# Attention with a written-out TensorE order, its transposes in two PSUM pools, and the bias sums one unit ahead

## The chip, the cores and the metric

The kernel runs on one core of one Trainium2 chip. The metric is device time in microseconds of one execution; less is better. A core has five engines that run side by side, each with its own queue of instructions in a fixed order: TensorE (PE: matrix products and transposes; PEld is its weight load), VectorE (DVE), ScalarE (ACT), GpSimd (POOL), and SyncE (SP), which here only starts DMA transfers. Work memory is SBUF; TensorE writes its results to PSUM, which has eight banks of 128 x 512 float32.

## What is computed

One layer of a streaming encoder on 1024 frames with width 1024, float32. Cut to what matters here:

```python
h = rmsnorm(x, pre_norm_mix) * (1.0 + scale_m) + shift_m
proj = h @ w_in            # q_lat, kv_lat, k_idx, w_idx, z, xbc, dt_raw, g_a, g_b
y_a = sparse_mla_attention(...) @ w_o_attn
y_b = ssd_mixer(z, xbc, dt_raw, ...) @ w_o_ssd
mix = (sigmoid(g_a) * y_a + sigmoid(g_b) * y_b) @ w_out
x = x + gate_m * rmsnorm(mix, post_norm_mix)
...
f = (silu(u_gate) * u_up) @ w_ffn_out
x = x + gate_f * rmsnorm(f, post_norm_ffn)
```

The attention has 16 heads. An indexer scores all keys for each query, the 256 best admissible keys are kept, and

```python
logits = einsum('bqhc,bqkc->bhqk', q_b, kv_sel) * scale + bias
probs = softmax(where(valid, logits, -inf))
o = einsum('bqhk,bqkc->bqhc', probs, kv_sel)
o = einsum('blhc,hcd->blhd', o, w_uv)
```

The xbc columns go through a causal convolution of four taps and a Silu before the state-space mixer. g_a and z are the columns of the two gates.

## The kernel before

The kernel is written against a framework that traces it in program order, then plans: a planner simulates the engines in time, gives an instruction that stands earlier in the program the higher priority, and so fixes each engine's queue at compile time. [...] `in_order(engines)` (line 103) chains the instructions traced inside it on the named engines, so that the planner must keep their program order there; other instructions may still be put between them. PSUM is split into a pool `ps` of five banks (`bank`) and a pool `pd` of three (`bank_d`).

The stages, in order: projections and the indexer's scores; the ranking, which finds the 256 best keys of each query by bisection on VectorE and ScalarE and writes the masks `mk` (line 700); attention; the state-space mixer; the merge of the two branches; the feed-forward part.

**Filler.** The remaining columns of w_in need nothing but h: 32 tiles of 128 columns for the convolution, 16 for z, 8 for g_a. One tile is 8 row tiles x 3 products (each float32 operand is split into a high and a low part) x 2 halves of the frames = 48 matmuls of 128x512 into the tile `pw` (line 224). The string FILL lists them: x or X a group of four convolution tiles, z and a one gate tile each. A convolution tile is read from PSUM by ScalarE (line 909) and three taps by VectorE (lines 912 to 914); a Silu follows on ScalarE (line 919). With X the Silus of two tiles are done together.

**Attention** is 8 head pairs (hp) times 4 units u of 256 queries, taken in the order u = 0, 2, 1, 3: 32 units. `att_scores` makes queries (`puq`, 12 matmuls; split into qh on ScalarE, line 735, and ql on VectorE, line 736). Then come four steps, one for each query tile t and head hh: GpSimd adds bias and mask into `nm` (line 748, once per t), TensorE makes scores into one or two banks `plg` (line 764), VectorE adds nm or mk and takes the maximum (line 773), ScalarE takes the exponential and its sum (line 776), VectorE the reciprocal (line 777). `att_out` of the unit before transposes the probabilities, one turn for each key tile j (`pt`, line 797), copies them to SBUF (`pc`: VectorE for odd j, ScalarE for even j), multiplies them with the values (`po`, line 813) and scales by the spread reciprocals (r2, lines 784 and 809). `weave` alternates steps of `att_scores` with steps of `att_out`. Beside each unit, `ada_next` makes one column of the modulation: weights `adaw` by DMA, products on GpSimd (lines 315, 316), a sum on VectorE (line 317), a small matmul `adap`.

In the program, hp 0 to 2 stand first, then FILL, then hp 3 to 7. No order is forced (`ATT_ORDER` is empty). Transposes of hp 0 to 2 take banks of `ps`, the later ones of `pd`.

Of the kernel before, what the change touches and what calls it, by code (L numbers as in the profile page):

```python
# [10 lines left out]
F32 = mybir.dt.float32  # L11
# [6 lines left out]
P = 128  # L18
# [12 lines left out]
LOWEST = -BIGGEST  # L31
QC = 256
ORDERED = (mybir.EngineType.PE, mybir.EngineType.Activation, mybir.EngineType.DVE)
FILL = "xxxxx" + "z" * 16 + "a" * 8 + "XXX"
HP_FIRST = 3
LEAD = 1.5
U_ORDER = (0, 2, 1, 3)
ATT_ORDER = ()
NCH = L // QC
EARLY = 18  # L40

# [24 lines left out]
def build(tc, a, dbg=None, stop=99, slots=None):  # L66
# [658 lines left out]

    qscale = KV_RANK ** -0.5

    def att_scores(u, uq, nb, out):

        pq = bank("puq")  # L730
        for hh in range(2):
# [9 lines left out]
        for t in range(2):  # L741
            i = 2 * u + t
            n = (i + 1) * P
            near = max(0, n - 256)
            nw = n - near
            nm = Q("nm", (P, 2, 256))
            mk = MK[i][:, near:n] if i in MK else dmask[:, 256 - nw:256]
            G.tensor_tensor(nm[:, :, 0:nw], nb[:, :, 256 - nw:256], mk[:, None, :].to_broadcast([P, 2, nw]), op=OP.add)
            a_ = max(256, n - 512) if n > 512 else 0
            for hh in range(2):  # L750
                st = [QQ[x][:, 256 * hh + 128 * t:256 * hh + 128 * t + 128] for x in range(2)]
                if u >= 2:
                    lg = R("lg")
                else:
                    if hh == 0:
                        pair = R("lg")
                    lg = pair[:, half(hh)]
                mx = sm.tile([P, 4], F32, name="mx", bufs=6)
                pb_ = {}
                for o_, w_ in ((a_, n - a_),) + (((0, a_),) if a_ else ()):  # L760
                    p = bank("plg")
                    w2 = max(w_, 256)
                    for x, (qi, ki) in enumerate(P3):
                        T.matmul(p[:, 0:w2], st[qi], KVT[ki][:, o_:o_ + w2], start=x == 0, stop=x == 2)  # L764
                    pb_[o_] = p
                parts = [(a_, near, n, nm[:, hh, 0:nw])]
                if near > a_:
                    parts.append((a_, a_, near, MK[i][:, a_:near]))
                if a_:
                    parts.append((0, 0, a_, MK[i][:, 0:a_]))  # L770
                m = 3e38
                for x, (o_, s_, e_, add) in enumerate(parts):
                    V.tensor_tensor_reduce(lg[:, s_:e_], pb_[o_][:, s_ - o_:e_ - o_], add, op0=OP.add, op1=OP.min,  # L773
                                           scale=-1.0, scalar=m, accum_out=mx[:, x:x + 1])
                    m = mx[:, x:x + 1]
                S.activation(lg[:, 0:n], lg[:, 0:n], AF.Exp, scale=-1.0, bias=m, accum_out=mx[:, 3:4])  # L776
                V.reciprocal(rr[:, 2 * t + hh:2 * t + hh + 1], mx[:, 3:4])
                out[hh, t] = lg
                yield

    def att_out(hp, u, vt, PR):

        r2 = sm.tile([P, 2, 2, 64], F32, name="r2", bufs=1)
        G.tensor_copy(r2, PR["rr"].rearrange("p (t h) -> p t h", t=2)[:, :, :, None].to_broadcast([P, 2, 2, 64]))
        po = bank("po")
# [4 lines left out]
        def turn(j):  # L790
            ts = (0, 1) if j < last else (1,)
            sl = slice(ts[0], 2)
            pt = (bank if hp < HP_FIRST else bank_d)("pt")
            ptv = pt.rearrange("p (h t n) -> p h t n", h=2, t=2)
            for hh in range(2):
                for t in ts:
                    T.transpose(ptv[:, hh, t, :], PR[hh, t][:, j * P:(j + 1) * P], ident)  # L797
            pc = Q("pc").rearrange("p (h t n) -> p h t n", h=2, t=2)
            if j % 2:
                V.tensor_copy(pc[:, :, sl], ptv[:, :, sl])  # L800
            else:
                S.activation(pc[:, :, sl], ptv[:, :, sl], AF.Copy)
            parts[j] = pc, sl
# [39 lines left out]

    att = {}

    def attention(steps, last, beside=lambda: None):

        for s_ in steps + [None] * last:
            nxt = iter(())
            if s_ is not None:  # L850
                hp, u = s_
                if u == U_ORDER[0]:
                    vt = vp.tile([P, NT, P], F32, name="vt", bufs=1)
                    SP.dma_start(vt, d_v[hp])
                    att["w"] = small_weights(a["w_uq"][hp]), vt, load_bias(hp)
                uq, vt, nb = att["w"]
                PR = {}
                nxt = att_scores(u, uq, nb, PR)
            prev = att.get("prev")
            if prev is None:  # L860
                weave(nxt, 5, iter(()), 0)
            else:
                weave(nxt, 5 if s_ else 0, att_out(*prev), 2 * prev[1] + 3, lead=LEAD)
            if s_ is not None:
                att["prev"] = (hp, u, vt, PR)
            beside()
# [3 lines left out]
    def ada_next():  # L870
# [3 lines left out]
            ada_col(*late.pop(0))  # L874
        if j is not None:
            late.append(ada_slow(j))

    if stop != 3:
        attention([(hp, u) for hp in range(HP_FIRST) for u in U_ORDER], 0, ada_next)
        if stop == 4:  # L880
            attention([(hp, u) for hp in range(HP_FIRST, 8) for u in U_ORDER], 1)
    if stop == 4:
        for k in range(KT):
            for b in BS:
                t = EV("attd")
                SP.dma_start(t, d_att[k][:, half(b)])
                dump("attn", t, (k, slice(None), half(b)))
        ctx.close()
        return


    def wide(c):
        W.plan(col_tile(a["w_in"][c]))
# [25 lines left out]
            S.activation(t, t, AF.Silu)  # L919
            SP.dma_start(dst, t)  # L920

    def conv_group(g, n):

        tiles = ((16 + g, d_bc[g, 0]), (24 + g, d_bc[g, 1]), (2 * g, d_xs[2 * g]), (2 * g + 1, d_xs[2 * g + 1]))
        for i in range(0, 4, n):
            outs = [o for t in tiles[i:i + n] for o in conv(*t)]
            if n > 1:
                with in_order(mybir.EngineType.Activation):
                    conv_out(outs[::-1])
            else:  # L930
                conv_out(outs)

    n_x, n_z, n_a = iter(range(GROUPS)), iter(range(16)), iter(range(8))
    for kind in FILL:
        if kind in "xX":
            conv_group(next(n_x), 2 if kind == "X" else 1)
        elif kind == "z":
            t = next(n_z)
            gate(1 + t, d_z[t], AF.Silu)
        elif stop != 3:  # L940
# [119 lines left out]
    def beside():  # L1060

        for t in range(8):
            W.plan(col_tile(a["w_in"][57 + t]))
            w = wpieces(ks8)
            for b in BS:
                p = bank_d("pw")
                yield from dense_steps(p, b, w, Hs)
                o = EV("g")
                S.activation(o, p, AF.Copy)
                SP.dma_start(d_gb[t][:, half(b)], o)  # L1070
                yield
        AT = [([None, None], [None, None]) for _ in range(KT)]
        for b in BS:
            for k in range(KT):
# [474 lines left out]
```

## Time and profile before

| | us |
|---|---|
| median of three runs | 2464.63 |
| the three runs | 2464.63, 2466.57, 2458.57 |
| the profiled execution, own time | 2461.74 |
| its span, first to last instruction | 2459.9 |
| mean granted TensorE clock in it | 0.985 |
| ranking's last mask written | 678.4 |
| first and last transposes of attention | 675.0, 1147.7 |

The page of the profile gives for each engine its busy time and share of the span, then the chain of work that ended last. A row of a window gives the stretch, its length, each engine's busy time with its number of instructions, and then PEclk, the share of the TensorE clock that was granted. A row of waits names who waited, for whom, and then the total us, the number of times, and the longest. A row of the timeline gives start and duration in us, engine, line, operation and out<-in, and in brackets the idle time before it with what ended it; matmuls of one line that follow one another are merged (x16). A row of groups gives count | busy us, mean ns of one | idle us before it and what ended that. Matmuls are pipelined, so their durations overlap: what one costs is read from start to start.

### The profile page before, as it was taken

The page shows a single profiled execution, that of the slowest core. Times are in us where ns is not written, and L with a number is a line of the kernel's source. Part 1 is how long each engine was busy: PE and PEld are TensorE (multiplying, and loading weights), DVE is VectorE, ACT ScalarE, POOL GpSimd, SP SyncE. Part 2 cuts the span into 40 slices and gives each one's busy share as a digit, 9 for nine tenths or more (in the row PEclk, how much of TensorE's full clock was granted, in tenths as well). Part 3 has the DMA queues.
Part 4 walks back from the last instruction along what each step waited for, and adds up shares of the span by engine and source line. Part 5 has one row for each costly group of instructions (what it writes and reads, how often), then busy time and mean ns, then how long its engine had stood idle before and what let it go on. Part 6 is the DMA issues. An engine that isn't in the chain of part 4 may idle for free.

```text
span 2459.9 us, 34979 instructions
## 1 busy us (share of the span) xinstructions
PE 2387.0 (97%) x11940; PEld 1933.8 (79%) x11940; DVE 1447.2 (59%) x2956; ACT 1209.1 (49%) x2327; POOL 1079.3 (44%) x877
## 2 busy tenths in 40 slices
PE   7999999999899999999999999999999999999997
PEld 5788888888788887777776777888777888888886
DVE  4566775599745656765558667365476666542211
ACT  3446665567444555555656555454454222344432
POOL 2722112222234344563335345656576555444564
PEclk8999999999999999999999999999999999999999
DMA  7224212522222332223668775664465444354453
GB/s 268 90 86 126 69 65 79 162 86 98 91 63 87 107 97 94 89 82 124 214 215 261 231 231 194 210 201 160 159 216 172 154 159 146 120 163 142 146 164 113
DMA packets 219746, 352.79 MB, mean 143 GB/s; under 512 B 22016, under 2 KB 86192, under 8 KB 219568
## 3 DMA queue, kind: packets, MB, share of 16 engines
q1 hardware_dynamic: 218848, 349.99, 44.1%
q8 instruction: 94, 1.54, 0.3%
q14 instruction: 84, 0.69, 0.1%
q10 hardware_dynamic: 720, 0.58, 0.1%
HBM read 266.31 MB, written 87.32 MB: 144 GB/s over the span
## 4 chain that ended last, share of the span: by engine, by line
PE 76%; DVE 9%; DMA 5%; ACT 4%; issue 3%; POOL 2%; SPq 1%; POOLq 0%; ACTq 0%; DVEq 0%
PE pw L224 17%; PE p L1281 14%; PE pfo L1413 9%; PE plg L764 4%; PE pos L224 4%; PE poa L234 3%; PE pot L224 3%; PE po L813 3%; PE pt L797 3%; PE pw L234 3%; PE prel L581 3%; PE puq L224 2%; DVE junk L634 2%; ACT junk L636 1%; PE pp L370 1%
## 5 line engine op out<-in xcount | busy, mean ns | idle before, releaser
L150 POOL TENSOR_TENSOR wlo<-wraw,whi 128x512 fp32r<-128x512 f32 x242 | 329.1, 1362 | 606.9 <-ACT whi L149 551.0
L1281 PE MATMUL p<-xh,wr 128*128 128x512 f32 x880 | 274.4, 391 | 3.1 <-DVE g L1331 3.1
L149 ACT ACTIVATE whi<-wraw 128x512 fp32r<-128x512 f32 x242 | 150.9, 626 | 195.0 <-issue 45.1
L1413 PE MATMUL pfo<-a,fwh 128*128 128x512 f32 (+1 forms) x684 | 208.6, 386 | 0.9 <-DVE a L245 0.9
L1275 POOL TENSOR_TENSOR wr<-a,wr 128x512 fp32r<-128x512 f32 x110 | 151.0, 1386 | 103.2 <-ACT wr L1274 70.4
L1281 PEld LDWEIGHTS p<-xh,wr 128*128 128x128 f32 x880 | 165.9, 189 | 38.0 <-DVE g L1331 3.5
L1281 PE MATMUL p<-xl,wr 128*128 128x512 f32 x440 | 171.7, 390 | 0.0
L245 POOL TENSOR_TENSOR fwl<-fw,fwh 128x512 fp32r<-128x512 f32 x92 | 113.4, 1236 | 115.9 <-ACT fwh L244 111.1
L1413 PEld LDWEIGHTS pfo<-a,fwh 128*128 128x128 f32 x684 | 127.5, 188 | 27.8 <-DVE a L245 1.8
L776 ACT ACTIVATE lg<-lg,mx 128x256 f32<-128x256 f32 (+7 forms) x128 | 98.2, 769 | 75.6 <-DVE mx L773 74.5
L1413 PE MATMUL pfo<-a,fwl 128*128 128x512 f32 (+1 forms) x342 | 131.8, 385 | 0.0
L1274 ACT ACTIVATE wr<-a 128x512 fp32r<-128x512 f32 x110 | 67.7, 628 | 123.3 <-PE p L1281 94.1
L315 POOL TENSOR_TENSOR adaw<-adaw,cs 128x512 f32<-128x512 f32 x64 | 66.7, 1043 | 117.9 <-DMA adaw<-ada_w 117.8
L244 ACT ACTIVATE fwh<-fw 128x512 fp32r<-128x512 f32 x92 | 54.5, 594 | 124.2 <-PE pfo L1413 95.5
L1281 PE MATMUL p<-h2h,wr 128*128 128x512 f32 x352 | 112.3, 396 | 0.0
L636 ACT ACTIVATE junk<-acc,cand__2203 128x1024 bf16<-128x1024 f32 (+2 forms) x96 | 86.2, 898 | 45.1 <-DVE cand__2203 L679 28.1
L224 PE MATMUL pos<-yw,whi 128*128 128x512 f32 x256 | 101.9, 398 | 3.3 <-DVE yw L1124 3.3
L224 PE MATMUL pos<-yh,whi 128*128 128x512 f32 x256 | 101.4, 396 | 2.9 <-ACT yh L1123 2.9
L224 PE MATMUL pos<-yh,wlo 128*128 128x512 f32 x256 | 101.5, 396 | 0.7 <-POOL wlo L150 0.7
L587 DVE SCALAR_TENSOR_TENSOR acc<-rel,widx,acc 128x384 f32<-128x384 f32 (+2 forms) x90 | 87.1, 988 | 24.5 <-ACT rel L582 24.3
L582 ACT ACTIVATE rel<-prel 128x512 f32<-128x512 f32 (+3 forms) x160 | 77.2, 524 | 47.7 <-PE prel L581 44.2
L1281 PEld LDWEIGHTS p<-xl,wr 128*128 128x128 f32 x440 | 83.0, 189 | 17.3
(567 smaller groups left out, 6869.1 us busy)
## 6 DMA issues: line engine op xcount, KB each, us to landing
wraw<-w_in SPq DMA_DIRECT2D x130, 256.0 KB, 2.9
a<-w_ffn_in SPq DMA_DIRECT2D x124, 256.0 KB, 3.3
fw<-w_ffn_out SPq DMA_DIRECT2D x80, 256.0 KB, 2.7
adaw<-ada_w SPq DMA_DIRECT2D x64, 256.0 KB, 2.8
al<-d_ac SPq DMA_DIRECT2D x32, 512.0 KB, 5.7
wraw<-w_o_ssd SPq DMA_DIRECT2D x64, 256.0 KB, 3.2
al<-d_a SPq DMA_DIRECT2D x44, 256.0 KB, 5.3
d_a<-g SPq DMA_DIRECT2D x40, 256.0 KB, 2.4
```

The lines of the kernel that those rows point to most:

```text
L149: behind(S.activation(hi[:, :kt], raw[:, :kt], AF.Copy))
L150: behind(G.tensor_tensor(lo[:, :kt], raw[:, :kt], f(hi[:, :kt]), op=OP.subtract))
L224: T.matmul(o, wt[:, k0 + i, :], xs[k][xi][b][:, sl], start=pi == 0 and i == 0 and wt is hi and xi == 0, stop=pi == len(pcs) - 1 and i == l ...
L234: T.matmul(o, wt[:, k0 + j, :], xs[k][xi][b], start=i == 0, stop=i == 23)
L245: (lo_eng or V).tensor_tensor(lo, src, f(hi), op=OP.subtract)
L587: V.scalar_tensor_tensor(acc[i][:, 0:n], rel[:, 0:n], ws, acc[i][:, 0:n], op0=OP.mult, op1=OP.add)
L636: S.activation(jk, y, AF.Sign, scale=-1.0, bias=a_, accum_out=o)
L764: T.matmul(p[:, 0:w2], st[qi], KVT[ki][:, o_:o_ + w2], start=x == 0, stop=x == 2)
L776: S.activation(lg[:, 0:n], lg[:, 0:n], AF.Exp, scale=-1.0, bias=m, accum_out=mx[:, 3:4])
L1275: G.tensor_tensor(w[:, 1], src, f(w[:, 0]), op=OP.subtract)
L1281: T.matmul(p, w[:, wi, i], X[x][i][xi], start=start and i == 0 and k == 0, stop=i == 3 and k == 2, skip_group_check=True)
L1413: T.matmul(p, w[wi][:, k - k0], xs[k][xi][:, sl], start=k == 0 and i == 0, stop=k == FT - 1 and i == 2)
```

## The change

Attention becomes one stretch of 32 units behind the filler, and TensorE's order in it is the program's. FILL loses its last three groups X (12 tiles, convolution groups 5 to 7). `woven` issues them in steps of six matmuls, three steps to a unit, through `conv_steps`; that handles one half of the frames at a time, in one pd bank, and takes the last three frames of the first half along in `ends`. Within a unit the order is: a step of scores, then a quarter of the turns of the unit before, and so on, then the last step of att_out; filler steps are spread evenly. Even turns j use a `pd` bank, odd ones a `ps` bank. VectorE copies the turns with j % 3 = 1, ScalarE the others. `biases` makes both sums of a unit while the unit before is running, with the load of the bias at the head pair's first unit. The exponential's sum goes straight into rr, and one reciprocal per unit replaces four.

```diff
-FILL = "xxxxx" + "z" * 16 + "a" * 8 + "XXX"
-HP_FIRST = 3
-LEAD = 1.5
+FILL = "xxxxx" + "z" * 16 + "a" * 8
+WOVEN = "XXX"
 U_ORDER = (0, 2, 1, 3)
-ATT_ORDER = ()
...
-    def att_scores(u, uq, nb, out):
+    def biases(hp, u):
+
+        if u == U_ORDER[0]:
+            att["nb"] = load_bias(hp)
+        out = []
+        for i in (2 * u, 2 * u + 1):
+            n = (i + 1) * P
+            nw = min(n, 256)
+            nm = Q("nm", (P, 2, 256))
+            mk = MK[i][:, n - nw:n] if i in MK else dmask[:, 256 - nw:256]
+            G.tensor_tensor(nm[:, :, 0:nw], att["nb"][:, :, 256 - nw:256], mk[:, None, :].to_broadcast([P, 2, nw]), op=OP.add)
+            out.append(nm)
+        return out
+
+    def att_scores(u, uq, nms, out):
...
-            nm = Q("nm", (P, 2, 256))
-            mk = MK[i][:, near:n] if i in MK else dmask[:, 256 - nw:256]
-            G.tensor_tensor(nm[:, :, 0:nw], nb[:, :, 256 - nw:256], mk[:, None, :].to_broadcast([P, 2, nw]), op=OP.add)
+            nm = nms[t]
...
-                S.activation(lg[:, 0:n], lg[:, 0:n], AF.Exp, scale=-1.0, bias=m, accum_out=mx[:, 3:4])
-                V.reciprocal(rr[:, 2 * t + hh:2 * t + hh + 1], mx[:, 3:4])
+                S.activation(lg[:, 0:n], lg[:, 0:n], AF.Exp, scale=-1.0, bias=m, accum_out=rr[:, 2 * t + hh:2 * t + hh + 1])
...
     def att_out(hp, u, vt, PR):
 
+        V.reciprocal(PR["rr"], PR["rr"])
...
-            pt = (bank if hp < HP_FIRST else bank_d)("pt")
+            pt = (bank if j % 2 else bank_d)("pt")
...
-            if j % 2:
+            if j % 3 == 1:
                 V.tensor_copy(pc[:, :, sl], ptv[:, :, sl])
...
-    def attention(steps, last, beside=lambda: None):
+    def attention(steps, beside, fill, nf):
 
-        for s_ in steps + [None] * last:
+        ahead = biases(*steps[0])
+        for n, s_ in enumerate(steps + [None]):
             nxt = iter(())
...
                 PR = {}
-                nxt = att_scores(u, uq, nb, PR)
+                nms, ahead = ahead, biases(*steps[n + 1]) if n + 1 < len(steps) else None
+                nxt = att_scores(u, uq, nms, PR)
             prev = att.get("prev")
-            if prev is None:
-                weave(nxt, 5, iter(()), 0)
-            else:
-                weave(nxt, 5 if s_ else 0, att_out(*prev), 2 * prev[1] + 3, lead=LEAD)
+            out, turns = (att_out(*prev), 2 * prev[1] + 2) if prev else (iter(()), 0)
+            order = [nxt]
+            for i in range(4):
+                order += [out] * (-(-(i + 1) * turns // 4) - order.count(out)) + [nxt]
+            order.append(out)
+            k = 0
+            for i, g in enumerate(order):
+                next(g, None)
+                while k < nf[n] and k * len(order) < nf[n] * (i + 1):
+                    next(fill, None)
+                    k += 1
...
-    if stop != 3:
-        attention([(hp, u) for hp in range(HP_FIRST) for u in U_ORDER], 0, ada_next)
...
+    def conv_steps(ch, dst, outs):
+
+        W.plan(col_tile(a["w_in"][17 + ch]))
+        w = wpieces(ks8)
+        ends = sm.tile([P, 3], F32, name="ends")
+        for b in BS:
+            p = bank_d("pw")
+            yield from dense_steps(p, b, w, Hs)
+            t = EV("cv")
+            S.activation(t, p, AF.Identity, bias=col("conv_b", ch), scale=col("cw3", ch))
+            if b == 0:
+                V.tensor_copy(ends, p[:, 509:512])
+            for s, nm_ in ((1, "cw2"), (2, "cw1"), (3, "cw0")):
+                c = col(nm_, ch)
+                V.scalar_tensor_tensor(t[:, s:], p[:, :512 - s], c, t[:, s:], op0=OP.mult, op1=OP.add)
+                if b:
+                    V.scalar_tensor_tensor(t[:, :s], ends[:, 3 - s:], c, t[:, :s], op0=OP.mult, op1=OP.add)
+            outs.append((t, dst[:, half(b)]))
+            yield
...
+    def woven():
+
+        for kind in WOVEN:
+            if kind == "a":
+                t = next(n_a)
+                yield from gate_steps(49 + t, d_sga[t])
             else:
-                conv_out(outs)
+                tiles = group_tiles(next(n_x))
+                for i in (0, 2):
+                    outs = []
+                    for t in tiles[i:i + 2]:
+                        yield from conv_steps(*t, outs)
+                    with in_order(mybir.EngineType.Activation):
+                        conv_out(outs[::-1])
...
-    if stop != 3:
-        with in_order(*ATT_ORDER):
-            attention([(hp, u) for hp in range(HP_FIRST, 8) for u in U_ORDER], 1, ada_next)
+    units = [(hp, u) for hp in range(8) for u in U_ORDER]
+    fill = woven()
+    with in_order(mybir.EngineType.PE):
+        attention(units, ada_next, fill, [3] * 33)
+        for _ in fill:
+            pass
```

`gate_steps` is the loop over one gate tile that stood in the state-space stage's `beside`, now a function; what it issues there is unchanged.

More of the change, by code (lines that the diff above doesn't have):

```diff
@@ L854, in attention @@
                     SP.dma_start(vt, d_v[hp])
-                    att["w"] = small_weights(a["w_uq"][hp]), vt, load_bias(hp)
-                uq, vt, nb = att["w"]
+                    att["w"] = small_weights(a["w_uq"][hp]), vt
+                uq, vt = att["w"]
                 PR = {}
-                nxt = att_scores(u, uq, nb, PR)
+                nms, ahead = ahead, biases(*steps[n + 1]) if n + 1 < len(steps) else None
+                nxt = att_scores(u, uq, nms, PR)
             prev = att.get("prev")
-            if prev is None:
-                weave(nxt, 5, iter(()), 0)
-            else:
-                weave(nxt, 5 if s_ else 0, att_out(*prev), 2 * prev[1] + 3, lead=LEAD)
+            out, turns = (att_out(*prev), 2 * prev[1] + 2) if prev else (iter(()), 0)
[9 more added lines that the diff above has]
+                    k += 1
             if s_ is not None:
@@ L876, in ada_next @@
             late.append(ada_slow(j))
-    if stop != 3:
-        attention([(hp, u) for hp in range(HP_FIRST) for u in U_ORDER], 0, ada_next)
[L880 to L889, printed above, removed]
     def wide(c):
@@ L920, in conv_out, with group_tiles @@
             SP.dma_start(dst, t)
[L922 to L929, printed above, removed]
-            else:
-                conv_out(outs)
+    def group_tiles(g):
+        return (16 + g, d_bc[g, 0]), (24 + g, d_bc[g, 1]), (2 * g, d_xs[2 * g]), (2 * g + 1, d_xs[2 * g + 1])
@@ new lines, in conv_group @@
+    def conv_group(g):
+        for t in group_tiles(g):
+            conv_out(conv(*t))
+    def conv_steps(ch, dst, outs):
[16 more added lines that the diff above has]
+            yield
@@ new lines, in gate_steps @@
+    def gate_steps(c, dst):
+        W.plan(col_tile(a["w_in"][c]))
+        w = wpieces(ks8)
+        for b in BS:
+            p = bank_d("pw")
+            yield from dense_steps(p, b, w, Hs)
+            t = EV("g")
+            S.activation(t, p, AF.Copy)
+            SP.dma_start(dst[:, half(b)], t)
+            yield
+    def woven():
[3 more added lines that the diff above has]
+                yield from gate_steps(49 + t, d_sga[t])
+            else:
+                tiles = group_tiles(next(n_x))
[5 more added lines that the diff above has]
+                        conv_out(outs[::-1])
@@ L933, in build @@
     n_x, n_z, n_a = iter(range(GROUPS)), iter(range(16)), iter(range(8))
     for kind in FILL:
-        if kind in "xX":
-            conv_group(next(n_x), 2 if kind == "X" else 1)
+        if kind == "x":
+            conv_group(next(n_x))
         elif kind == "z":
@@ L939, in build @@
             gate(1 + t, d_z[t], AF.Silu)
-        elif stop != 3:
+        else:
             t = next(n_a)
             gate(49 + t, d_sga[t], AF.Copy)
-    if stop != 3:
-        with in_order(*ATT_ORDER):
-            attention([(hp, u) for hp in range(HP_FIRST, 8) for u in U_ORDER], 1, ada_next)
+    units = [(hp, u) for hp in range(8) for u in U_ORDER]
[4 more added lines that the diff above has]
+            pass
     for _ in range(35):
@@ L1062, in beside @@
         for t in range(8):
[L1063 to L1071, printed above, removed]
+            yield from gate_steps(57 + t, d_gb[t])
         AT = [([None, None], [None, None]) for _ in range(KT)]
```

## Prediction, made before the changed kernel was built or run

> **What bounds the kernel now.** I read the page first: span, engine shares, the chain.
>
> ```profile
> span 2459.9 us, 34979 instructions
> PE 2387.0 (97%) x11940; PEld 1933.8 (79%) x11940; DVE 1447.2 (59%) x2956; ACT 1209.1 (49%) x2327; POOL 1079.3 (44%) x877
> PE 76%; DVE 9%; DMA 5%; ACT 4%; issue 3%; POOL 2%; SPq 1%; POOLq 0%; ACTq 0%; DVEq 0%
> ```
>
> TensorE is busy 97% of the span and carries 76% of the chain; VectorE and ScalarE are far from full. So a change pays here in three ways only: TensorE waits less, runs less of its time at half clock, or does the same matmuls in fewer nanoseconds. The change keeps every matmul. Next come the windows around attention, then the waits of TensorE in the stretch 930 to 1155.
>
> ```profile
> core 0: us, PE busy (x) PEld busy (x) DVE busy (x) ACT busy (x) POOL busy (x), PEclk, DMA share, GB/s
> 668.00:675.00 7.00, 0.82 (x4) 0.35 (x2) 7.00 (x13) 0.52 (x3) 0.00 (x0) 0.71 0.00 0
> 675.00:681.00 6.00, 5.97 (x20) 5.01 (x21) 3.40 (x13) 2.58 (x8) 2.92 (x4) 0.50 0.03 3
> 681.00:930.00 249.00, 249.00 (x1407) 204.20 (x1407) 136.54 (x426) 120.85 (x226) 94.49 (x90) 1.00 0.28 89
> ...
> 940.00:948.00 8.00, 5.94 (x35) 5.15 (x31) 3.14 (x9) 5.86 (x9) 4.01 (x4) 0.79 0.73 220
> 948.00:1128.00 180.00, 175.62 (x1241) 135.34 (x1239) 128.59 (x505) 97.02 (x222) 104.82 (x107) 1.00 0.28 86
> ```
>
> ```profile
> PE plg L764 <- DVE mx L773: 4.0, 4, 1.0
> ```
>
> Three losses are visible: one gap at 668 to 675 with the clock at 0.50 behind it (between 681 and 930 TensorE is busy for all of the 249 us), one of 2.1 us at 940 to 948 (8.00 - 5.94, clock 0.79), and four of 1.0 us in the stretch where attention runs alone. A fourth does not count as idle: the order of the matmuls.
>
> **The change part by part.**
>
> *The first gap.* The filler in front of attention is now 44 column tiles of 48 matmuls, 2112 in all.
>
> ```profile
> 80.00:668.50 588.50, 486.38 (x2041) 1.00 0.30 98
> ```
>
> ```profile
> 701.05 3.64 PE pw L224 x16
> ```
>
> ```profile
> 675.03 0.48 PE L797 MATMUL pt<-ident,lg 128*128 128x128 f32 x1 [6.21 <-ACT lg L776]
> ```
>
> ```profile
> 677.97 0.43 DVE L700 TENSOR_SCALAR mk<-run 128x512 bf16<-128x512 f32 x1
> ```
>
> Up to the gap (the window of tile pw, x2041) 71 matmuls fewer than that are done, because hp 0 to 2 stand ahead of the filler in the program and their transposes went into TensorE's queue while VectorE was still making the masks (last one at 677.97, third fence). A filler matmul takes 3.64 / 16 = 0.2275 us (a row of the chain), so the 71 fill 16.2 us: TensorE is fed to 668.6 + 16.2 = 684.8, past the last mask. The idle 6.2 goes, and so do the 3.0 lost in 6.0 us at clock 0.50: **9.2**. The cover is the 16.2 us of filler; were it used up earlier, the 9.2 comes back whole. What is late next is the first unit's softmax, and VectorE has been free for 6 us by then.
>
> *Sums of bias and mask one unit ahead.*
>
> ```profile
> 1007.40 2.28 POOL L748 TENSOR_TENSOR nm<-nb,mk 128x512 f32<-128x512 f32 x2
> ```
>
> ```profile
> 1009.05 0.42 DVE L800 COPY pc<-pt 128x256 f32<-128x256 f32 x1 [1.85 <-PE pt L797]
> 1009.39 0.41 DVE L773 CUSTOM_DVE_ANT_0 lg<-plg,nm 128x256 f32<-128x256 f32 x1
> ```
>
> ```profile
> 1010.70 0.47 PE L764 MATMUL plg<-kvth,qh 128*128 128x512 f32 x1 [0.99 <-DVE mx L773]
> ```
>
> This is one of the four 1.0 us waits. TensorE waits for a score bank; VectorE's read of it starts at 1009.39, behind a copy that itself waited 1.85 for transposes. GpSimd's first sum ends at 1007.40 + 1.14 = 1008.5, the second at 1009.7, so at the place where VectorE took the copy the read had no sum yet. A unit ahead, the sums have some 14 us of slack and the read can go first; that VectorE's new order does so is my assumption, not shown. The work stays 2 x 1.14 us per unit; it moves past the r copy and the adaw products of the unit in GpSimd's queue, neither of which is needed before the unit's end, and the nb load moves ahead of vt and uraw in SyncE's. Gain **4.0** (0 to 4.0).
>
> *The fixed order.* In the old order the value products (po) are cut into pieces.
>
> ```profile
> PEld po L813 <- issue: 12.7, 71, 0.4
> ```
>
> ```profile
> 1002.23 0.65 PE L813 MATMUL po<-pc,vt 128*64 128x256 f32 x4
> 1002.81 0.38 PE L224 MATMUL puq<-qnh,uh 128*128 128x256 f32 x1
> 1003.03 0.28 PE L224 MATMUL puq<-qnl,uh 128*128 128x256 f32 x1
> ...
> 1004.35 0.38 PE L797 MATMUL pt<-ident,lg 128*128 128x128 f32 x2
> 1004.66 0.44 PE L813 MATMUL po<-pc,vt 128*64 128x128 f32 x4
> 1005.03 1.31 PE L797 MATMUL pt<-ident,lg 128*128 128x128 f32 x10
> ```
>
> ```profile
> 749.99 0.38 PE L809 MATMUL po<-ident,r 128*128 128x128 f32 x2
> 750.29 3.46 PE L813 MATMUL po<-pc,vt 128*64 128x256 f32 x32
> 753.69 0.38 PE L284 MATMUL adap<-ones,adas 128*128 128x1 f32 x2
> ```
>
> Between 680 and 1155 the weight loader pauses 71 times on entering po; attention has 32 units, and the new att_out issues all po matmuls of a unit in one step that the TensorE order keeps together: 32 entries. The price of an entry comes from starts. In the long run 32 matmuls take 753.69 - 750.29 = 3.40, or 0.425 per turn of four. A turn of four alone takes 1002.81 - 1002.23 = 0.58, and the first puq behind it steps 0.22, where the other eleven take 1004.35 - 1003.03 = 1.32, 0.12 each; on entry the two transposes at 1004.35 take 0.31, while ten at 1005.03 take 1.06, 0.11 each, so 0.09 more. Extra: 0.58 - 0.425 + 0.10 + 0.09 = 0.345; for the short turn at 1004.66, 0.37 alone, nearer 0.25. With 0.32, the 39 entries fewer are worth **12.5** (9.8 to 13.5, or nothing if other TensorE work still cut the runs, which the fixed order excludes).
>
> *The 2.1 us wait* came from ScalarE changing tables for the filler's Silu:
>
> ```profile
> 939.86 1.28 ACT L919 ACT_TABLE_LOAD   x1 [3.07 <-DVE mod L285]
> ...
> 941.15 2.19 ACT L919 ACTIVATE cv<-cv 128x512 f32<-128x512 f32 x4
> ...
> 943.51 0.58 ACT L735 ACTIVATE qh<-puq 128x512 fp32r<-128x512 f32 x1
> ...
> 944.15 0.69 PE L764 MATMUL plg<-kvth,qh 128*128 128x384 f32 x1 [2.06 <-ACT qh L735]
> 944.60 1.28 ACT L776 ACT_TABLE_LOAD   x1
> ```
>
> With the clock at 0.79 over 8 us the episode cost 2.1 + 1.7 = **3.8**. [...] I count 3.8 as removed, and enter its successors as an addition.
>
> *What it adds.* Six such ScalarE blocks remain (three X groups, two each); one lasts 1.28 + 2.19 + 1.28 = 4.7 us. Behind puq the new order puts one filler step (6 x 0.2275 = 1.4) and a turn of transposes (four at 0.11), 1.8 us, then plg, which needs qh. Queued behind a late qh are ql on VectorE, and on TensorE everything.
>
> ```profile
> L735 ACT ACTIVATE qh<-puq 128x512 fp32r<-128x512 f32 x17 | 10.0, 587 | 14.5 <-PE puq L224 14.5
> ```
>
> This group of the stretch 948 to 1128 counts 17 units. A unit will last about 14.1 us: 180.0 / 17 = 10.6 (the stretch by its units), less 0.4 of po and 0.2 of waits, plus three filler steps, 4.1. A block of 4.7 us falls on a qh in one case of three: two of six, at 3.8, **7.6** (0 to 22.8).
>
> The filler's convolution now comes in 24 halves, each with three long VectorE steps (one row for six alike).
>
> ```profile
> L912 DVE SCALAR_TENSOR_TENSOR cv<-pw,vec,cv 128x511 f32<-128x511 f32 x12 | 9.0, 748 | 9.8 <-ACT cv L909 9.8
> ```
>
> Such a chunk, 3 x 0.75 = 2.2 us, delays VectorE's score reads and with them score banks; pw also holds one of three pd banks, which the even transposes share. Only u = 3 waited for a bank before, 1.0 each. A quarter of 24 halves: **6.0** (0 to 24). VectorE gets 128.59 / 17 = 7.6 plus 12 tiles x 6 x 0.75 / 32 = 1.7, so 9.3 of 14.1 us or 66%; alone it was 71% (128.59 of 180). Three reciprocals fewer per unit, and 7 copies of 20 instead of 10, only lower that; the copies go to ScalarE, 54% alone (97.02 of 180). No engine but TensorE is the bound.
>
> Sum: 9.2 + 4.0 + 12.5 + 3.8 = 29.5 removed, 7.6 + 6.0 = 13.6 added, net 15.9. Behind attention TensorE stays the engine that sets the end, so the end moves by as much. The profiled execution took 2461.7 us (span 2459.9 and 1.8 around it), 2.9 below the median 2464.6. **2461.7 - 15.9 = 2445.8, say 2446.**
>
> **The rivals.** *No new stall:* the waits of the stretch alone, at 71% VectorE, were 4.4 us in 180, and almost all are the sums'. Then 2461.7 - 29.5 = 2432. Against it: the stretch alone has no table change.
>
> *The gain is given back:* each of the six blocks hits (22.8) and bank waits come at 0.3 per half (7.2): 30.0, against 29.5. Time 2462. For it: a fixed order cannot slip a filler matmul into a wait; the old one had filler at hand from 681 to 930, and no wait.
>
> *The filler does not reach:* the planner spends the 44 tiles before VectorE is ready, and the 9.2 stays: 2446 + 9.2 = 2455.
>
> *Slower:* plg waits for qh in every unit, because the planner puts an exponential or a copy ahead of qh on ScalarE. Place: between puq and the first plg; cover 1.8 us, need 0.58 and hand-over, so 0.9 of other work ahead of it is enough. The price seen is 2.06: 32 x 2.06 = 66, hence 2461.7 - 29.5 + 66 = 2498. It decides from 29.5 / 32 = 0.9 us per unit on (1.2 for slower by 0.3%). Against it: in the stretch alone, qh waits for puq and not the reverse.
>
> [...]
>
> **How the numbers follow.** About what a measurement of this kernel can tell from no change is 0.3%, 7.4 us. Forecast 0.55 (2438 to 2454), no new stall 0.16, filler does not reach 0.05, gain given back 0.12, slower 0.10, micro-idling 0.02. The forecast and no new stall are faster by over 7.4: 0.71. The filler case and the gain given back lie within: 0.17. Slower: 0.12. The range runs from 2428, no new stall with po at its upper price and some slack, to 2464, the gain given back; it leaves out the slow cases and the edges.
>
> **What would show it.** Right: no wait of pt for lg near 670 and no half clock there; no nm among VectorE's releasers; po entries near 32; TensorE's waits in attention below 14 us, with qh and mx as releasers next to table loads and cv steps. Wrong: a row "plg <- qh" with some thirty counts; waits of pt for pc, which would say that the shared pd banks bind; granted clock below 1.00 inside attention; or an end of attention that came earlier while the state-space stage behind it starts no sooner.

## The result, and the profile after

| | before | after |
|---|---|---|
| median of six runs, us | 2462.76 | 2446.73 |
| the profiled execution, own time, us | 2461.74 | 2446.71 |
| last value product of attention, us in the trace | 1152.9 | 1134.2 |
| runs of value products on TensorE in attention | 86 | 34 |

The ratio of after to before is 0.9937, 95% interval 0.9925 to 0.9949: faster by 0.6%, some 15 us. The forecast was 2446. From the page of the changed kernel, its span, the engine shares and the chain:

```profile
span 2444.9 us, 34790 instructions
PE 2374.4 (97%) x11940; PEld 1938.1 (79%) x11940; DVE 1434.9 (59%) x2848; ACT 1225.8 (50%) x2351; POOL 1081.3 (44%) x877
PE 60%; DVE 4%; DMA 3%; ACT 2%; issue 2%; POOL 2%; SPq 0%; DVEq 0%; POOLq 0%; ACTq 0%
```

The 11940 matmuls are the same, and TensorE is busy for 12.6 us less (2387.0 to 2374.4): which fits value products in longer runs and the half clock behind the first gap (0.50 over 6.0 us) being gone. The shares of the chain add up to 73% here, since it could be followed back only to 676.65; they can't be set against the 76% of before. So I go by windows and waits. First the windows of the changed kernel, ahead of attention and across it:

```profile
640.00:680.00 40.00, 38.46 (x170) 31.50 (x170) 34.05 (x45) 8.28 (x14) 12.92 (x9) 1.00 0.26 85
681.00:1134.00 453.00, 444.16 (x2887) 367.63 (x2887) 285.60 (x906) 258.02 (x525) 205.99 (x204) 0.99 0.30 93
```

The first gap and the half clock behind it are gone: in 640 to 680 only 1.5 us are idle, at clock 1.00. In attention TensorE idles 8.8 of 453 us, with VectorE at 63% and ScalarE at 57%. Its waits there, and the weight loader's pauses before the value products (who waits, for whom, total us, times, longest):

```profile
PE pt L807 <- ACT lg L786: 5.0, 6, 1.1
PE plg L774 <- ACT qh L747: 1.9, 2, 0.9
PE plg L774 <- DVE ql L748: 0.6, 1, 0.6
PE pt L807 <- ACT pc L812: 0.4, 1, 0.4
PE plg L774 <- DVE mx L783: 0.4, 1, 0.4
PE plg L774 <- DVE pc L810: 0.3, 1, 0.3
```

```profile
PEld po L823 <- issue: 4.7, 27, 0.4
```

Five of the 8.6 us are transposes (pt) that wait for the last exponential (lg) of their unit. The wait for a score bank (mx), 4.0 before, is 0.4. The pauses fell from 71 to 27.

What makes lg late stands in ScalarE's timeline of the changed kernel at one of its six table-load blocks:

```profile
823.26 1.28 ACT L924 ACT_TABLE_LOAD   x1
824.55 2.20 ACT L924 ACTIVATE cv<-cv 128x512 f32<-128x512 f32 x4
826.77 1.28 ACT L786 ACT_TABLE_LOAD   x1
828.06 0.72 ACT L786 ACTIVATE lg<-lg,mx 128x512 f32<-128x512 f32 x1
...
829.57 0.58 ACT L747 ACTIVATE qh<-puq 128x512 fp32r<-128x512 f32 x1
```

And in TensorE's at the same place:

```profile
827.39 0.49 PE L807 MATMUL pt<-ident,lg 128*128 128x128 f32 x3
828.93 0.33 PE L807 MATMUL pt<-ident,lg 128*128 128x128 f32 x1 [1.05 <-ACT lg L786]
830.20 0.50 PE L774 MATMUL plg<-kvth,qh 128*128 128x512 f32 x1 [0.94 <-ACT qh L747]
```

The block, 823.26 to 828.06, holds up the unit's last exponential. The fourth transpose waits 1.05 for it; qh, which stands behind two further steps of ScalarE, holds the next unit's first score matmul for 0.94. Two windows of the changed kernel, at that place and right behind it:

```profile
827.00:831.00 4.00, 2.01 (x10) 1.02 (x8) 1.29 (x3) 3.62 (x7) 1.66 (x3) 1.00 0.77 267
831.00:835.00 4.00, 4.00 (x14) 3.46 (x15) 2.15 (x7) 0.37 (x1) 2.29 (x3) 0.57 0.38 111
```

1.99 us idle, and then clock 0.57 over 4 us, which loses another 1.7. The same happens at 1053 (1.09 and 0.94 us of waits, then clock 0.63 over 1057 to 1061); the other blocks cost a wait without the clock (1.00 over 757 to 765, 898 to 908 and 984 to 992), or, in one case of six, nothing.

### The profile page after: what moved, and what is told of

It is laid out like the page before. It is cut to its first block, busy times and chain, and to the rows that moved or that the text cites. A ratio compares the mean times of both kernels' runs of the same rounds, so it can differ in the third digit from the quotient of the medians.

```text
span 2444.9 us, 34790 instructions
## 1 busy us (share of the span) xinstructions
PE 2374.4 (97%) x11940; PEld 1938.1 (79%) x11940; DVE 1434.9 (59%) x2848; ACT 1225.8 (50%) x2351; POOL 1081.3 (44%) x877
## 4 chain that ended last, share of the span: by engine, by line
PE 60%; DVE 4%; DMA 3%; ACT 2%; issue 2%; POOL 2%; SPq 0%; DVEq 0%; POOLq 0%; ACTq 0%
PE p L1324 14%; PE pfo L1456 9%; PE pw L232 8%; PE pos L222 5%; PE plg L774 4%; PE poa L232 3%; PE pot L222 3%; PE po L823 2%; PE pt L807 2%; PE puq L222 2%; PE pyd L1071 1%; PE pst L1078 1%; DMA a<-w_ffn_in 1%; PE pcb L1027 1%; PE pyo L1083 1%
```

## The experiments

Each run is given as a ratio to the kernel before with its 95% interval; where I say "against after", I take the two ratios' difference times 2462. "Excess" is what TensorE's starts in attention show beyond the steps of the undisturbed runs of each kind of matmul and the price of entering po: waits, half clock, and whatever else makes a step long. It is added up over some 2900 starts of a trace, so it has no row of its own: 23.4 us before, 19.8 after. It is an estimate: its level depends on which steps are taken as undisturbed (idle time in attention and the loss by half clock alone are 8.8 + 3.4 = 12.2 us after), and its differences between runs are firmer than its level. A profile shows one execution, which can lie some us off the median that the ratio rests on.

### x1_fill_ahead: the 44 filler tiles ahead of hp 0 to 2, alone

```diff
-FILL = "xxxxx" + "z" * 16 + "a" * 8 + "XXX"
+FILL = "xxxxx" + "z" * 16 + "a" * 8 + "1XXX"
...
-    if stop != 3:
-        attention([(hp, u) for hp in range(HP_FIRST) for u in U_ORDER], 0, ada_next)
...
+        if kind == "1":
+            attention([(hp, u) for hp in range(HP_FIRST) for u in U_ORDER], 0, ada_next)
```

> The kernel before, with the first 44 filler tiles moved ahead of hp 0 to 2 in the program; nothing else. Theory (the gap behind the ranking is worth 9.2 us by itself): no wait of pt for lg near 670, no half clock there, 8 to 10 us faster than before. Rival (the gap only moves, because filler that is used up earlier is missing beside hp 0 to 2): within 3 us of before, with new waits between 680 and 930.

Measured: 0.9973 (0.9962 to 0.9983), 6.6 us faster than before. Windows of this kernel at the old gap and behind it:

```profile
668.00:675.00 7.00, 7.00 (x32) 5.79 (x32) 5.94 (x8) 1.15 (x3) 3.38 (x2) 1.00 0.45 150
675.00:681.00 6.00, 6.00 (x34) 5.20 (x33) 0.41 (x1) 2.81 (x5) 2.13 (x4) 1.00 0.36 131
681.00:930.00 249.00, 246.41 (x1417) 202.01 (x1417) 144.89 (x457) 129.41 (x245) 96.33 (x93) 0.99 0.27 88
```

The gap and its half clock are gone entirely, as predicted: 7.00 of 7 us busy where it was 0.82. But the stretch behind it, busy for all of its 249 us before, now has 2.6 us of waits: attention in the old order has less filler around it. In the trace attention ends 8.3 us earlier (1144.6 for 1152.9). So the 9.2 is there, and some of it is paid back, which leaves less than the 8 to 10 us expected.

### x2_sums_ahead: the sums one unit ahead, alone

```diff
+        ahead = biases(*steps[0])
+        for n, s_ in enumerate(steps + [None] * last):
...
+                nms, ahead = ahead, biases(*steps[n + 1]) if n + 1 < len(steps) else None
+                nxt = att_scores(u, uq, nms, PR)
```

> The kernel before, with the sums of bias and mask made one unit ahead; nothing else. Theory of the prediction (the sums are late, and the planner puts the score read first once they are not): the four waits of 1.0 us of plg for mx go, 4 us faster. Rival (VectorE's order behind a copy is the cause, and a free order keeps it): the four waits stay, within 1 us of before.

Measured: 0.9978 (0.9967 to 0.9988), 5.4 us faster than before. Of the waits from 640 to 1180 this one is the only row above 1.2 us:

```profile
PE plg L776 <- DVE ql L750: 8.6, 1, 8.6
```

It is the first gap, which this kernel keeps. No row plg <- mx is left, so with the sums at hand VectorE's score reads do come in time: the assumption of the prediction holds. The 5.4 us are not this term alone, though. No row plg <- qh is left either, so the 2.1 us wait behind the filler's table load is gone in this kernel too, and with it, I take it, its half clock (3.8 together), while its first gap is 2.4 us longer (8.6 for 6.2): 4.0 + 3.8 - 2.4 would make 5.4.

### x5_order_only and x3_free_order: the written-out order alone, and all but it

x5 is the kernel before with its own program order forced on TensorE from hp 3 on; x3 is the changed kernel with the order left to the planner.

```diff
-ATT_ORDER = ()
+ATT_ORDER = (mybir.EngineType.PE,)
```

```diff
-    with in_order(mybir.EngineType.PE):
+    if True:
```

> The kernel before, with TensorE's order fixed to the program's in the attention of hp 3 to 7 (20 of 32 units); the weave, banks, sums and filler as before. Theory (a value product cut off costs 0.32 us, and 71 entries become one per unit there): some 24 entries fewer, 7 to 8 us gained on po, less what the rigid order adds in waits; 0 to 8 us faster. Rival (the order is worth nothing by itself, the even filler is): entries fall and the time does not, or it grows by 5 us or more through waits of plg for qh, since no filler step stands behind puq here.

> The changed kernel without the fixed TensorE order: the planner places the same program. Theory: the value products are cut again (60 entries or more by the weight loader's pauses, against 27), 8 to 13 us lost on them; some of the waits behind table loads are filled by the planner, 0 to 6 us won back: 4 to 12 us slower than the changed kernel, and still 4 to 12 us faster than before. Rival (the gain came from the filler's places and the gap alone): within 2 us of the changed kernel.

Measured: x5 1.0033 (1.0022 to 1.0044), 8.1 us slower than before; x3 0.9988 (0.9976 to 1.0001), 12.6 us slower than after. x5 enters po 42 times instead of 86 (some 24 fewer were expected), and pays for that in waits (640 to 1180), as its rival had it:

```profile
PE adap L284 <- DVE mx L773: 8.2, 5, 2.0
PE pt L797 <- ACT lg L776: 8.1, 5, 6.2
PE plg L764 <- ACT qh L735: 6.6, 11, 2.3
```

The pt row holds the first gap, 6.2. The plg row is the rival "plg waits for qh" in the old code: without a filler step behind puq nothing covers qh, 11 times. x5's rows add up to 23.8 us, for 13.3 before. In the profiled execution, the fastest of its twelve, waits and saved entries nearly cancel: attention ends 2.3 us later than before, so the trace does not show all of the 8.1 us. x3, in the same stretch:

```profile
PE pt L807 <- ACT lg L786: 9.1, 4, 4.2
...
PEld po L823 <- issue: 5.0, 30, 0.2
```

Left free, the planner still keeps the po products together (39 runs; 30 pauses), where 60 entries or more were expected. So forcing the order isn't what takes the entries away: the new `att_out`, which issues a unit's products in one step, does that by itself. What the forced order brings over x3 is fewer and shorter waits (x3's rows add up to 18.9 us from 640 to 1180, those of after to 10.1), and no 6.8-us stretch of half clock, of which x3 has two; at clock 0.50 they lose 6.8 us, where after loses 3.4.

### x4_no_tables: the filler's 12 tiles without a table change

This kernel leaves out the Silu of the 12 woven tiles (a copy takes its place).

```diff
-                        conv_out(outs[::-1])
+                        conv_out(outs[::-1], AF.Copy)
```

> The changed kernel with the Silu of the 12 woven tiles replaced by a copy, so that ScalarE loads no table inside attention (the Silu of those tiles is left out). Theory (five of the six blocks of two table loads and four Silus hold up the exponentials, and TensorE's waits and two half-clock windows come from them): the waits in attention fall from about 9 us to under 3, no half clock inside attention, 8 to 12 us faster than the changed kernel. Rival (the waits come from the rigid order as such): they stay at two thirds or more, under 4 us faster.

Measured: 0.9899 (0.9884 to 0.9914), 9.4 us faster than after. Its window of attention, and its waits there:

```profile
681.00:1123.00 442.00, 440.47 (x2896) 367.04 (x2896) 285.28 (x906) 246.28 (x516) 206.44 (x205) 1.00 0.30 96
```

```profile
PE plg L774 <- DVE ql L748: 0.9, 2, 0.5
PE plg L774 <- DVE mx L783: 0.3, 1, 0.3
PE plg L774 <- DVE pc L810: 0.3, 1, 0.3
```

ScalarE loads one table (1.28 us) between 681 and 1120. Both pt <- lg and plg <- qh are gone, all half clock too (1.00 over the window), and attention is 13.1 us shorter (683.8 to 1123.1, after 681.8 to 1134.2). Excess falls from 19.8 to 6.7. The six blocks, 12 table loads of 1.28 us in all, are the one cost of size that the change adds.

### x6_one_pool: all transposes in the three pd banks

```diff
-            pt = (bank if j % 2 else bank_d)("pt")
+            pt = bank_d("pt")
```

> The changed kernel with all transposes in the three pd banks, which they share with pw. Theory (pd has one bank left for transposes while a filler half is read out, so two pools are needed): waits of pt for pc and of pw for pt appear, 5 to 20 us slower than the changed kernel. Rival (the second pool is worth nothing, since a unit's copies come fast enough): within 2 us.

Measured: 0.9960 (0.9945 to 0.9975), 5.7 us slower than after; the intervals just overlap (0.9945 to 0.9949). Its row from 640 to 1180 that after has at 0.4:

```profile
PE pt L807 <- ACT pc L812: 4.5, 5, 1.9
```

With pw in one of the three banks, transposes wait for copies. Using both pools is worth about these 4 us, likely and not certain.

### x7_none_woven and x8_clustered: where the filler's steps stand

x7 puts all 56 tiles ahead of attention, x8 gives six steps to the unit in which a block of Silus falls due, and two or three to the others.

```diff
-FILL = "xxxxx" + "z" * 16 + "a" * 8
-WOVEN = "XXX"
+FILL = "xxxxx" + "z" * 16 + "a" * 8 + "XXX"
+WOVEN = ""
...
+        elif kind == "X":
```

```diff
-        attention(units, ada_next, fill, [3] * 33)
+        attention(units, ada_next, fill, [6, 2, 3, 2, 3] * 6 + [1, 0, 0])
```

> The changed kernel with all 56 filler tiles ahead of attention and none woven in. Theory (the filler step behind puq is the cover of qh, 1.8 us with it and 0.4 without): plg waits for qh in most units, 0.5 to 1 us each, 10 to 30 us of waits, against the 10 us that the table loads cost now: 0 to 20 us slower than the changed kernel. Rival (the filler in attention brings only its table loads): no such waits, 8 to 12 us faster.

> The changed kernel with the same 96 filler steps spread 6, 2, 3, 2, 3 over units in turn, so that the unit in which a block of table loads and Silus falls has six steps. Theory (more filler in that unit covers ScalarE's 4.7 us): the waits behind the blocks fall by half or more, 3 to 8 us faster than the changed kernel. Rival (the waits fall where the block ends, behind the unit's filler): no change within 2 us.

Measured: x7 1.0008 (0.9997 to 1.0019), 17 us slower than after: the whole gain is gone, with one whole table block amid the transposes (at 820.31) instead of six. The order of the program is not quite that of the trace: the last filler runs behind the first scores (first plg at 704.3, first pt at 812.9). Two of its rows (640 to 1180):

```profile
PE plg L774 <- ACT qh L747: 7.3, 15, 0.6
PE pt L807 <- ACT lg L786: 5.8, 10, 3.3
```

15 short waits for qh, in about half of the 32 units, and ten for lg, of which the longest, 3.3, is the one block's: in after the filler step covers most of them. That is the slower rival's mechanism, with 0.5 us instead of 2.06 for each. All its rows add up to 18.6 us, for 10.1 after. That accounts for the profiled execution, which at 2454.74 is the fastest of its twelve and only 8.0 us above after's (granted clock 0.992 in it, 0.985 to 0.990 in the other eleven). Where the other 9 us of the median come from, this trace does not show.

x8: 0.9923 (0.9906 to 0.9941), 3.4 us faster than after, with intervals that overlap; and pt <- lg is 6.4 in six waits, plg <- qh 2.3 in three, no less than after. The predicted cause is not there; this run is inconclusive.

### y1_long_blocks: three table blocks of eight Silus instead of six of four

```diff
-                for i in (0, 2):
-                    outs = []
-                    for t in tiles[i:i + 2]:
-                        yield from conv_steps(*t, outs)
+                outs = []
+                for t in tiles:
+                    yield from conv_steps(*t, outs)
```

> The changed kernel with the Silus of all four tiles of a woven group done together: three blocks of two table loads and eight Silus (6.9 us) instead of six of four (4.8 us). Theory (a wait is what a block leaves over beyond TensorE's cover of 2 to 4 us): six waits of some 2 us become three of some 4 us, each with half clock behind it; ScalarE saves 7.7 us that nobody waited for: within 4 us of the changed kernel. Rival (each table load costs TensorE its length): half the loads, 5 to 8 us faster.

Measured: 0.9945 (0.9931 to 0.9958), no difference from after that can be told (2 us). In its waits (640 to 1180):

```profile
PE pt L807 <- ACT lg L786: 6.7, 3, 3.1
```

Two of the three blocks cost a wait of some 3 us (2.9 at 826.7 and 3.1 at 983.8), each followed by a shorter one and by half clock (0.62 and 0.57 over some 4 us behind them); the third, at 1126.65, cost none. Half the loads in longer blocks bring nothing, which fits that what counts is how long ScalarE is away from the exponentials at one time (4.80 us in the block of after shown above; 6.9 was reckoned here).

### y2_po_cut: each turn's po products two turns behind its transposes

```diff
         for j in range(last + 1):
...
+            if j > 1:
+                product(j - 2)
...
-        for j in range(last + 1):
-            pc, sl = parts.pop(j)
```

> The changed kernel with each turn's value products issued two turns later instead of all at the unit's end, in the same fixed order: about four entries into po per unit instead of one, near 128 instead of 34, the same matmuls. Theory (an entry costs TensorE 0.31 us of switching): 94 entries more, 25 to 31 us slower than the changed kernel, so 10 to 16 us slower than before. Rival (what looked like a price of the entry was another wait, and the order of the matmuls is free): within 4 us of the changed kernel, by waits on pc alone.

Measured: 1.0084 (1.0071 to 1.0098), 36 us slower than after, more than the 25 to 31 expected. It enters po 128 times instead of 34. One entry in its timeline:

```profile
910.26 0.38 PE L807 MATMUL pt<-ident,lg 128*128 128x128 f32 x2
910.57 0.65 PE L818 MATMUL po<-pc,vt 128*64 128x256 f32 x4
911.15 0.50 PE L774 MATMUL plg<-kvth,qh 128*128 128x512 f32 x1
911.48 0.39 PE L774 MATMUL plg<-kvtl,qh 128*128 128x512 f32 x1
911.71 0.40 PE L774 MATMUL plg<-kvth,ql 128*128 128x512 f32 x1
```

Four po products take 0.58 from start to start, for 0.425 in a long run. The first plg behind them steps 0.33, the next 0.23; the two transposes ahead take 0.31, for 0.22. That is 0.155 + 0.10 + 0.09 = 0.345 per entry, the same sum as in the prediction, and 94 entries make 32 us. Over all starts of the trace the entries come to some 34 to 36 us, 0.36 to 0.38 each, by the steps that are taken as undisturbed; a few us more are excess.

### y3_exp_silu and y4_tanh_silu: the Silu from a function that needs no other table

Both form the Silu of the woven tiles in place: y3 as x / (1 + exp(-x)), y4 as x (0.5 + 0.5 tanh(x / 2)). The multiplication goes to GpSimd. The core of y4; y3 has Exp with scale -1, an addition of 1 and `V.reciprocal` instead:

```diff
-                    with in_order(mybir.EngineType.Activation):
-                        conv_out(outs[::-1])
+                    for o, dst in outs:
+                        e = EV("e")
+                        S.activation(e, o, AF.Tanh, scale=0.5)
+                        V.tensor_scalar(e, e, 0.5, 0.5, op0=OP.mult, op1=OP.add)
+                        G.tensor_tensor(o, o, e, op=OP.mult)
+                        SP.dma_start(dst, o)
```

> The changed kernel with the Silu of the 12 woven tiles made as x / (1 + exp(-x)), for which ScalarE keeps the table that the softmax uses: an exponential on ScalarE, an addition and a reciprocal on VectorE, a product on GpSimd, tile by tile. Theory (the table loads are what the kernel without them gained 9 us by): no waits behind blocks, no half clock; VectorE gets 24 x 1.5 us more work in 450 us, which costs 0 to 5 us in score banks: 4 to 9 us faster than the changed kernel, 20 to 25 us faster than before. Rival (VectorE and GpSimd become late for scores, transposes and pw banks): within 3 us of the changed kernel or slower, with waits of plg for mx and of pt for pc.

> As y3_exp_silu, but the Silu of the 12 woven tiles is x (0.5 + 0.5 tanh(x / 2)): a tanh on ScalarE, which needs no other table than the softmax, 0.41 us on VectorE instead of 0.41 + 3.34, and the product on GpSimd (1.28 us). Theory (the reciprocals of 3.34 us made y3_exp_silu late, and the table loads are what the changed kernel still pays): like the kernel without tables, 6 to 10 us faster than the changed kernel, 21 to 26 us faster than before; no half clock in attention and no long wait of pt for lg. Rival (tile by tile in place of blocks, or GpSimd's products, hold up the rest): 0 to 4 us faster than the changed kernel.

Measured: y3 1.0136 (1.0122 to 1.0149), 49 us slower than after. From its groups of attention, and its waits:

```profile
L981 DVE RECIPROCAL e<-e 128x512 f32<-128x512 f32 x24 | 80.2, 3344 | 0.1
```

```profile
PE plg L774 <- DVE ql L748: 13.9, 3, 4.8
PE pt L807 <- ACT lg L786: 11.8, 8, 3.9
PE plg L774 <- DVE pc L810: 10.1, 4, 2.6
```

ScalarE loads one table between 681 and 1183, but each reciprocal takes VectorE for 3.34 us, where 1.5 was reckoned for it and the addition together (an estimate of mine that no run had shown), and what TensorE needs from VectorE comes late, by up to 4.8 us. Behind these waits half clock comes back: the granted clock over 681 to 1183 is 0.96, which loses some 20 us of the 502.

y4: 0.9917 (0.9905 to 0.9930), 4.9 us faster than after, the lowest ratio of all that compute the whole layer; its interval just overlaps after's (0.9925 to 0.9949). That is less than the theory's 6 to 10 us. Its waits:

```profile
PE plg L774 <- DVE mx L783: 5.6, 4, 1.7
PE plg L774 <- DVE ql L748: 3.3, 3, 1.2
...
PE puq L222 <- DVE mx L783: 0.8, 4, 0.3
```

Tanh took no table load of its own here: between 681 and 1131 ScalarE loads a table once, at attention's first exponential (683.54), and there is no half clock (1.00 over these 450 us). About half of x4's 9.4 us is got. The waits are no shorter than after's (9.7 us in these three rows, for 8.6); what the traces show as gained is the half clock, which lost after 3.4 us. The other half likely goes to VectorE, whose additional step (24 of them, 0.72 us on average where 0.41 was reckoned) and tap chunks now hold up the score reads (mx) and ql.

## Why the prediction was right, step by step

The predicted net gain was 15.9 us; the profiled executions differ by 15.0, the medians by 16.0. By terms:

- **First gap, 9.2:** right but for 1.5 us, and the cover was there (x1). One small thing was missed. The first sums of bias and mask stand in GpSimd's queue ahead of the last filler weights. From GpSimd's timeline of the changed kernel, and then TensorE's:

```profile
672.53 2.85 POOL L736 TENSOR_TENSOR nm<-nb,mk 128x512 f32<-128x512 f32 x2 [12.18 <-DVE mk L698]
675.35 3.75 POOL L148 TENSOR_TENSOR wlo<-wraw,whi 128x512 fp32r<-128x512 f32 x3
```

```profile
676.65 0.50 PE L222 MATMUL pw<-h4h,wlo 128*128 128x512 f32 x1 [1.54 <-POOL wlo L148]
```

  GpSimd stands for 12.18 us before sums that need VectorE's masks, and the weight's low part (wlo) behind them comes 1.5 us late. The prediction listed what the sums pass in GpSimd's queue inside a unit, and not this first pair. That the queue order is the cause is read from these rows; it was not tried apart.
- **Sums ahead, 4.0:** right; the row plg <- mx falls from 4.0 to 0.4, and to nothing in x2, whose 5.4 us hold other terms besides.
- **Entries into po, 12.5:** the price was right, the count was not. Counted by instruction, there were 86 runs before and 34 after, 52 fewer; from start to start the po products and the steps around them fell by some 16 to 18 us, or 0.31 to 0.34 each, by the steps that are taken as undisturbed. I had taken the weight loader's 71 pauses for the number of entries, but that row misses some: after, it has 27 for 34 runs. And the reason given, that "the fixed order excludes" other cuts, is not the one that counts: x3 has 39 runs without it.
- **The 2.1-us wait, 3.8:** gone with its block, as counted.
- **Table-load blocks, 7.6:** the mechanism was right, the place and the size were not. I let a block hit only the wait of plg for qh, in "two of six". In four of the six it first hits one of the unit's last exponentials, for which the last transposes wait, and five of six blocks cost something. By excess, x4 puts them at 13.1 us in attention; by the times at 9.4.
- **Bank waits from the convolution, 6.0:** hardly any; 0.4 for mx. The second pool for odd transposes (x6) and the sums ahead likely leave enough slack. They come when VectorE gets more to do (y4: 5.6).

The two additions together were predicted as 13.6, and came to 13.1 + 0.4 (9.4 + 0.4 by the times): the errors cancel, which is luck. Excess fell by 3.6 (17.0 removed, 13.6 added, would be 3.4), po by 16 or more where 12.5 stood, so attention ends 18.7 us earlier and not 15.9 (the two make 19.7 or more; the last us is not accounted for). Of this 15.0 reach the end. That the surplus on po and the loss behind attention nearly cancel is luck as well. The stages behind attention take 1310.7 us from the last po, and 1307.0 before. The prediction's "the end moves by as much" is the step that fails here, by 3.7. Windows of attention's output product (poa) and of the state-space output stage (pos to pot), before and then after:

```profile
1306.00:1469.00 163.00, 160.49 (x854) 122.74 (x854) 118.76 (x171) 94.01 (x207) 75.12 (x56) 0.97 0.75 237
1469.00:1768.00 299.00, 288.34 (x1285) 232.47 (x1286) 164.30 (x194) 149.23 (x265) 172.86 (x128) 0.98 0.55 182
```

```profile
1288.50:1445.00 156.50, 154.90 (x825) 119.27 (x825) 112.96 (x168) 91.36 (x201) 71.11 (x55) 0.98 0.74 235
1445.00:1750.50 305.50, 292.76 (x1316) 235.71 (x1316) 162.23 (x199) 152.83 (x271) 175.72 (x129) 0.98 0.55 184
```

The second stage takes 6.5 us longer, with 31 matmuls more, and the first 6.5 us less, with 29 fewer: work has moved across their border, and together they take 462.0 us both times. The loss lies on either side of them: 1.5 us right behind attention (153.0 before, 154.5 after, with 11 matmuls more) and 2.5 us from the last pot to the first product of the feed-forward output (430.0, 432.5). Right behind attention something can be seen: before, the planner had put the state-space stage's first product (pcb) at 1146.8, 6.1 us ahead of the last po; after, it stands at 1135.1, 0.9 behind it. So that stage starts 11.7 us sooner where attention ends 18.7 sooner, which is in part the last of the prediction's signs of being wrong. In the thirteen profiles of changed kernels, y4 and y1 among them, the stretch from the last po to the end lies between 1302 and 1313 us, whatever was edited in attention. So I take the 3.7 as scatter of the planner; which step of it decides was not tried.

Of the rivals, "the filler does not reach" is refuted, "no new stall" is about what x4 shows (2434.53, for 2432), and the slower one shows in kind where the filler's steps are taken away (x7). Half clock behind short waits, which has 0.02 among the chances, shows in part: both stretches of half clock in after (0.57 over 831 to 835, 0.63 over 1057 to 1061) follow two waits of about 1 us close together, at two of six blocks and not in every unit. Granted clock below 1.00 inside attention did appear, twice, which I had listed as a sign against; it belongs to the table blocks, since it goes with them in x4 and y4 (1.00 over 681 to 1123 and over 681 to 1131).

## What to carry to other kernels

Work woven into a matmul stream is worth something as cover: the kernel was 17 us slower when the same 12 tiles stood ahead of attention, and the 8 us of it that the trace shows are waits of TensorE for ScalarE and VectorE, which had no cover then. Before weaving, look at what the woven work does on the side engines: here a function from another table took ScalarE away for 4.8 us at a time (after, 823.26 to 828.06), and whether another form of it stays in the table, at what price on the next engine, is worth one run (y4 with tanh was 4.9 us faster than after, y3 with exp and a reciprocal 49 us slower). And count switches between kinds of matmul in the instruction list, not from pauses.

## What the hardware showed unexpectedly

- A reciprocal of 128x512 float32 on VectorE took 3.34 us in y3, eight times the 0.41 to 0.43 us that most of the additions of the same shape beside it took there (their mean is 0.54).
- Half clock for some 3.4 us came behind waits much shorter than the 6.2 us of the first gap, but these runs show no fixed limit. It followed one wait of 2.06 us (before, at 942; clock 0.58 over 944.1 to 948), two of about 1 us with one transpose between (after, at 828 and at 1054; 0.57 and 0.63 over the 4 us behind them), and 1.6 us in three pieces within 3.1 us (y2, from 762.9). It did not follow 1.5 us in three pieces (after, from 757.6 and from 983.6; 1.00 in the windows behind), nor single waits of 1.98 us (x8, from 1099.2), 2.49 (y3, from 1003.7) and 3.05 (x3, from 674.9). In y1 it followed each of the two waits of 2.9 and 3.1 us that have a shorter one behind them (0.62 and 0.57 over some 4 us).
- Entering and leaving a run of 64-column value products cost TensorE 0.3 to 0.4 us in starts here (0.345 in the entry shown in y2), though no engine waits for another in that time.
